# Two-layer decoder trunk on one core: heads and rests of the tokens in one 512-column product

## The chip, the cores and the metric

The kernel runs on one core of one Trainium2 chip. The metric is the device time of one execution in microseconds; the kernel before takes 1001.32 us, the median of three runs (1001.05 to 1001.64).

TensorE (PE in the profile) multiplies: a weight load (PEld) puts a 128x128 stationary operand in place, and a matmul then streams the columns of a moving operand past it into a bank of PSUM. VectorE (DVE), ScalarE (ACT) and GpSimd (POOL) work on tiles; SyncE (SP) and GpSimd issue the transfers from HBM.

## The reference

A trunk of two layers over 512 tokens of 1024 features, all float32. Layer 0 mixes tokens by causal pooling, layer 1 by dilated windowed attention; each is followed by a SwiGLU block, and the end is one more norm.

```python
for i in range(DEPTH):                    # 2
    h = rmsnorm(x, norm_mix[i])
    x = x + (pool_mixer(h, ...) if i % 2 == 0 else attn_mixer(h, ...))
    h = rmsnorm(x, norm_ffn[i])
    x = x + swiglu(h, ffn_w_gate[i], ffn_w_up[i], ffn_w_down[i])
return rmsnorm(x, norm_final)

def swiglu(h, w_gate, w_up, w_down):      # 1024 -> 2816 -> 1024
    g = jnp.einsum('bsd,df->bsf', h, w_gate)
    u = jnp.einsum('bsd,df->bsf', h, w_up)
    return jnp.einsum('bsf,fd->bsd', jax.nn.silu(g) * u, w_down)
```

The change lies in `swiglu`, in both layers.

## The kernel before, in words

**Heads and rests.** A float32 operand is kept as two parts that TensorE takes: the head `hi`, the value rounded, and the rest `lo`, what is left. A product of two operands is three matmuls: head by head, head of the weights by rest of the tokens, rest of the weights by head of the tokens. The weights are split on the chip: `weights` (L120) loads a tile of 128x1024 into `wraw` or `vraw` (L105; L107 adds a second piece in the transfer), casts it on ScalarE (L139) into `whi` and subtracts on VectorE (L143) into `wlo`. Split tiles live in a ring of five (`wspl`), and `weights` keeps about four products ahead. L145 adds raw tiles to each other.

**Seven products instead of eight.** The block of gate and up (1024 features, 512 tokens) is cut in two by two: features in two halves, tokens in two halves of 256. Instead of eight half-size products there are seven, over sums and differences of the quarters of the weights and of the tokens (a scheme like Strassen's, in Winograd's form); `RIGHT[i]` is the tokens' operand of product i. The seven results are combined in three sums: `p` collects products 0, 2, 4 and 6, `r` 1 and 5, `q` 3. `Group` is 256 of the 2816 inner features, gate and up together; there are eleven groups a layer. `Group.product` (L614) runs for g in gate, up and four chunks c of the features the three matmuls of L625, each with 256 columns, one PSUM bank holding gate in one half and up in the other: 24 matmuls. `done` (L632) takes the result out: product 0 to `keep`, 1 and 2 to tile `ct` (ScalarE, L636 to L640), 3, 4, 5 added or subtracted (VectorE, L642 to L646), then SiLU and the multiplication (L647 to L650; L653 and L658 for product 6). `first_half` and `second_half` make from `ct` the seven sums `u` that the down product wants and split them (L320, L321).

**Down.** `down(b)` (L696) takes a block of three groups (`BLOCKS`) through the same seven products, of tokens' halves by halves of the output columns: for two blocks t of 128 tokens each, nine matmuls of 512 columns (L712), 18 a product. After each product VectorE adds the accumulators to the residual stream `x` or subtracts them (L719, L721). The last block of two groups (9, 10) is multiplied plainly (L766).

**The order.** TensorE's order is the order in which the code is written (`manual_schedule`). `FFN_ORDER` gives it: groups 0 and 1 interleaved (`TWO`), groups 2 and 3, down 0, groups 4 to 6, down 1, groups 7 to 9, down 2, group 10, the last block. `enqueue_ffn` puts the weights in a queue in the same order, and loads go out on SP in that order. The other engines' instructions are ordered when the program is built, by priority: what takes results out of PSUM stands ahead (`URGENT`), products 5 and 6 less so (100).

**PSUM.** Four banks rotate under the name `mm`; two each are `p` and `r`, so the next group's `p` and `r` are others than this group's.

Of the kernel before, what the change touches and what calls it, by code (L numbers as in the profile page):

```python
# [10 lines left out]
F32 = mybir.dt.float32  # L11
# [35 lines left out]
FFN_ORDER = (  # L47
    [("two", 0)] + [("quad", n) for n in (2, 3)] + [("down", 0)]
    + [("quad", n) for n in (4, 5, 6)] + [("down", 1)] + [("quad", n) for n in (7, 8, 9)] + [("down", 2)]
    + [("quad", 10)] + [("last", 3)]  # L50
)

TWO = [(g, i) for g in (0, 1) for i in (0, 3)] + [(g, i) for i in (1, 2, 4, 5, 6) for g in (0, 1)]
# [5 lines left out]
def trunk_kernel(ctx: ExitStack, tc: tile.TileContext, x_in, xT, gam, gains, consts, ident_d, w0, wT, w1, wv, w_down, out):  # L59
# [15 lines left out]
    mm = ctx.enter_context(tc.tile_pool(name="mm", bufs=4, space=bass.MemoryType.PSUM))  # L75
# [92 lines left out]
    def enqueue_ffn(layer):  # L168
# [27 lines left out]
        def down(b):  # L196
            pairs = BLOCKS[b]
            at = layer * (NF // 2) + pairs[0]
            dn[b] = [{}, {}]
            for i in range(7):  # L200
                for js, a, n in zip(dn[b], (at, at + 2), (2, len(pairs) - 2)):
                    operand(js, i, lambda m, k: tiles[k, :, a : a + n, COLS[m]], (n, S), 10)

        for step, n in FFN_ORDER:
            if step == "two":
                for g, i in TWO:
                    quad(n + g, i, 5)
            elif step == "quad":
                for i in range(7):
                    quad(n, i)  # L210
            elif step == "down":
                down(n)
            else:
                dn[n] = [rows_of(w_down)(layer * NF + 2 * pair, half) for pair in BLOCKS[n] for half in range(2)]
# [27 lines left out]
    h_both = [stat.tile([P, NC * S + 2 * SHIFT], F32R, name=f"h_{part}") for part in ("hi", "lo")]  # L242

    def tokens_at(shift):
        return [h[:, shift : shift + NC * S].rearrange("p (c s) -> p c s", c=NC) for h in h_both]
# [105 lines left out]
    def out_projection(js, where, hi, lo, norm, shift, four, tps, hook=None):  # L351
# [22 lines left out]
        ws = [weights(js[4 + i], split_ahead=4 + i, load_ahead=6 + i) for i in range(4)]  # L374
        for b in range(4):
# [20 lines left out]
    with ExitStack() as pctx:  # L396
# [137 lines left out]

        third = out_projection(j_out, BY_GROUP, z_hi, z_lo, norm, SHIFT, [mm.tile([P, S], F32, name="mm") for _ in range(4)], turned_banks, lambda: group_products(1, early))

    def ffn(layer, norm, third, nxt):
# [8 lines left out]
        with ExitStack() as fctx:  # L546
# [5 lines left out]
            fps = open_pool("ffps", 2, space=bass.MemoryType.PSUM)  # L552
            early_u = open_pool("ffa", 2)
            third_chain = norm.chain.ins
            h_hi, h_lo = tokens_at(SHIFT)
            block = lambda t, k, n: t[:, 4 * k : 4 * k + 4, HALVES[n]]

# [3 lines left out]
            t2, t3, t4 = ([fp.tile([P, 4, 256], F32R, name=f"t_{part}{i}") for part in ("hi", "lo")] for i in (2, 3, 4))  # L561
            fp.tile([P, SHIFT], F32, name="gap3")
            T_hi, T_lo = ([block(h, 0, 1), t2[i], t3[i], t4[i]] for i, h in enumerate((h_hi, h_lo)))
            RIGHT = (
                [(block(h_hi, 0, 0), block(h_lo, 0, 0))] + [(T_hi[i], T_lo[i]) for i in (0, 1)]
                + [(block(h_hi, 1, 0), block(h_lo, 1, 0)), (T_hi[2], T_lo[2])]
                + [(block(h_hi, 1, 1), block(h_lo, 1, 1)), (T_hi[3], T_lo[3])]
            )
# [12 lines left out]
            class Group:  # L581


                def __init__(self, n, ct):
                    self.n, self.ct, self.sums = n, ct, {}
                    self.lst = ct.rearrange("p m n g c -> p (m n g) c")
                    pool = early_u if n % 4 < 2 else late_u[0]
                    self.u = u_of[n] = [pool.tile([P, 7, 256], F32R, name=t) for t in ("u_hi", "u_lo")]

                def first_half(self):  # L590

                    (hi, lo), lst = self.u, self.lst
# [21 lines left out]
                def product(self, i):  # L614
                    if i == 3:
                        self.sums["q"] = mm.tile([P, S], F32, name="mm").rearrange("p (g c) -> p g c", g=2)
                    elif i < 2:
                        self.sums["pr"[i]] = fps.tile([P, 2, 256], F32, name="pr"[i])
                    ps = self.sums["prpqprp"[i]]
                    whi, wlo = weights(gu[self.n][i])  # L620
                    hi, lo = RIGHT[i]
                    for g in range(2):
                        for c in range(4):
                            for k, (w, xx) in enumerate(((whi, hi), (whi, lo), (wlo, hi))):
                                nc.tensor.matmul(  # L625
                                    ps[:, g, :], lhsT=w[:, g, c, :], rhs=xx[:, c, :],
                                    start=i in (0, 1, 3) and g + c + k == 0, stop=c == 3 and k == 2, skip_group_check=True,
                                )
                    with tc.high_priority(URGENT if i < 5 else 100):
                        self.done(i)  # L630

                def done(self, i):  # L632
# [12 lines left out]
                    elif i == 5:  # L645
                        nc.vector.tensor_add(ct[:, 0, 1], r, ct[:, 0, 1])  # L646
                        nc.scalar.activation(ct[:, 0, :, 0, :], ct[:, 0, :, 0, :], AF.Silu)  # L647
                        nc.vector.tensor_mul(ct[:, 0, :, 0, :], ct[:, 0, :, 0, :], ct[:, 0, :, 1, :])
                        nc.scalar.activation(ct[:, 1, 1, 0, :], ct[:, 1, 1, 0, :], AF.Silu)
                        nc.vector.tensor_mul(ct[:, 1, 1, 0, :], ct[:, 1, 1, 0, :], ct[:, 1, 1, 1, :])  # L650
                        self.first_half()
# [42 lines left out]
            r_tile = lambda: by_four(fps.tile([P, 2, 256], F32, name="r").rearrange("p g c -> p (g c)"))  # L694

            def down(b):  # L696

                pairs = BLOCKS[b]

                p, r = ([fps.tile([P, 2, 256], F32, name=t).rearrange("p g c -> p (g c)") for _ in range(2)] for t in "rp")  # L700
                q = [mm.tile([P, S], F32, name="mm") for _ in range(2)]
                where = (0, 1, 2, 3, 6, 5, 4)
                target = ((0, 0, 1), (1, 1, -1), (0, 1, 1), (0, 0, 1), (1, 1, -1), (0, 1, 1), (1, 0, -1))
                for i, acc in enumerate((p, r, p, q, p, r, p)):
                    ws = [weights(js[i], held=z) for z, js in enumerate(dn[b])]
                    half, n, sign = target[i]
                    for t in range(2):
                        for c, pair in enumerate(pairs):
                            whi, wlo = (w[:, c % 2, :] for w in ws[c // 2])
                            hi, lo = (u[:, where[i], t * P : (t + 1) * P] for u in u_of[pair])  # L710
                            for k, (u, w) in enumerate(((hi, whi), (hi, wlo), (lo, whi))):
                                nc.tensor.matmul(  # L712
                                    acc[t], lhsT=u, rhs=w, start=i in (0, 1, 3) and c + k == 0,
# [3 lines left out]
                        with tc.high_priority(URGENT):  # L717
                            if sign > 0:
                                nc.vector.tensor_add(to, acc[t], to)  # L719
                            else:  # L720
                                nc.vector.tensor_sub(to, to, acc[t])  # L721

            for kind, n in FFN_ORDER[:-1]:
                if kind == "two":
                    groups = [Group(n, ct_common), Group(n + 1, ct_tile(hn, "ct_second"))]
                    with tc.issue_after(third_chain):
                        first_tokens(0, t1r)
                        first_tokens(1, b21r)
                    for at, (g, i) in enumerate(TWO):
                        if at in (0, 2):  # L730
                            b = 2 + at // 2
                            if b == 2:
                                late_banks[b] = third
                                norm.prepare(3, COLS)
                            else:
                                late_banks[b] = [r_tile(), by_four(mm.tile([P, S], F32, name="mm"))]
                                for half in range(2):
                                    norm.turn(b, half, late_banks[b][half])
                            late(b, 1)
                        if at in (4, 6, 8):  # L740
                            for b in (2, 3):
                                late(b, at // 2)
                        groups[g].product(i)
                    held.close()
                    late_u.append(open_pool("ffb", 2))
                elif kind == "quad":
                    group = Group(n, ct_common)
                    for i in range(7):
                        group.product(i)
                else:  # L750
                    down(n)
# [18 lines left out]
            junk = fps.tile([P, 2, 256], F32, name="p").rearrange("p g c -> p (g c)")  # L770
# [476 lines left out]
```

## Time and profile before

| what | value |
|---|---|
| median of three runs | 1001.32 us |
| the profiled execution | 1000.84 us |
| its span, first to last instruction | 999.0 us |
| TensorE matmuls, weight loads | 6575, 6575 |
| TensorE busy | 990.7 us, 99% |
| VectorE busy | 784.6 us, 79% |
| ScalarE busy | 529.5 us, 53% |
| granted TensorE clock | 0.999 |
| feed-forward of layer 0, of layer 1 | about 115 to 450 us, 663 to 999 us |
| gate and up (L625), matmuls in the two layers | 3696, of 256 columns |
| down by blocks (L712), matmuls in the two layers | 756, of 512 columns |

Busy times of matmuls overlap, since matmuls are pipelined: the time that one costs in a row of many is the distance of the starts, not its own length. The chain that ended last gives these distances: a piece such as "x24" is 24 matmuls of one product one behind the other, with its length.

### The profile page before, as it was taken

The numbers are of one execution on the slowest core, as the hardware profiler recorded it, in microseconds if no ns is written. First come the engines' busy times: TensorE is split into PE (matmuls) and PEld (weight loads), VectorE is DVE, ScalarE is ACT, GpSimd is POOL, SyncE is SP. The second block draws the span as 40 slices with busy tenths as digits, with TensorE's granted clock in tenths as the row PEclk, the third lists the DMA queues.
The fourth block names the chain that finished last, engine by engine and source line by source line (L and its number), as shares of the span: only waits on it lengthen the run. The fifth ranks groups of instructions, "written<-read, shape, count | busy, mean of one in ns | idle before, by whom it ended". The sixth has DMA issues, their size and how long they took to land.

```text
span 999.0 us, 16591 instructions
## 1 busy us (share of the span) xinstructions
PE 990.7 (99%) x6575; PEld 908.5 (91%) x6575; DVE 784.6 (79%) x1116; ACT 529.5 (53%) x838; POOL 113.1 (11%) x114
## 2 busy tenths in 40 slices
PE   9999999999999999999999999999999999999997
PEld 8888999989989998989888899899998998999896
DVE  6475799898888888777887557479989889788875
ACT  5573666545644554573543544356654554455354
POOL 0002010110011100002112024101011100111000
PEclk9999999999999999999999999999999999999999
DMA  9457277668559755524211249427666855975522
GB/s 334 177 168 190 60 197 177 151 187 233 149 126 292 182 137 148 183 76 135 83 58 53 62 153 284 92 64 196 174 158 200 234 148 123 289 179 138 155 67 84
DMA packets 76461, 157.29 MB, mean 157 GB/s; under 512 B 5904, under 2 KB 6288, under 8 KB 76384
## 3 DMA queue, kind: packets, MB, share of 16 engines
q1 hardware_dynamic: 58000, 121.00, 36.2%
q0 software_dynamic: 18096, 34.98, 20.3%
q8 instruction: 51, 0.84, 0.3%
q10 hardware_dynamic: 288, 0.27, 0.1%
q14 instruction: 26, 0.21, 0.1%
HBM read 154.08 MB, written 2.13 MB: 156 GB/s over the span
## 4 chain that ended last, share of the span: by engine, by line
PE 97%; ACT 1%; DMA 1%; DVE 1%; POOL 0%; issue 0%; DVEq 0%; ACTq 0%
PE p L625 25%; PE r L625 13%; PE r L712 10%; PE mm L625 6%; PE p L712 5%; PE mm L766 4%; PE mm L227 4%; PE mm L229 4%; PE mm L228 4%; PE mm L712 2%; PE early L443 2%; PE mm L363 2%; PE mm L361 2%; PE mm L362 2%; PE early L490 1%; PE tp L955 1%
## 5 line engine op out<-in xcount | busy, mean ns | idle before, releaser
L139 ACT CAST whi<-wraw 128x1024 fp32r<-128x1024 f32 (+2 forms) x189 | 184.9, 981 | 186.7 <-issue 45.8
L143 DVE TENSOR_TENSOR wlo<-wraw,whi 128x1024 fp32r<-128x1024 f32 (+2 forms) x190 | 221.1, 1165 | 76.2 <-ACT whi L139 75.7
L139 ACT CAST whi<-vraw 128x1024 fp32r<-128x1024 f32 (+1 forms) x102 | 99.6, 977 | 144.8 <-DVE vraw L145 53.7
L625 PE MATMUL p<-t_hi,wlo 128*128 128x256 f32 x528 | 149.8, 284 | 0.0
L625 PE MATMUL p<-t_lo,whi 128*128 128x256 f32 x528 | 149.4, 283 | 0.0
L625 PE MATMUL p<-t_hi,whi 128*128 128x256 f32 x528 | 148.4, 281 | 0.0
L143 DVE TENSOR_TENSOR wlo<-vraw,whi 128x1024 fp32r<-128x1024 f32 (+1 forms) x102 | 114.9, 1127 | 14.0 <-ACT whi L139 13.7
L625 PEld LDWEIGHTS p<-t_hi,whi 128*128 128x128 f32 x528 | 100.0, 189 | 0.0
L625 PE MATMUL r<-h_hi,wlo 128*128 128x256 f32 x352 | 99.9, 284 | 0.0
L625 PEld LDWEIGHTS p<-t_hi,wlo 128*128 128x128 f32 x528 | 99.6, 189 | 0.0
L625 PE MATMUL r<-h_lo,whi 128*128 128x256 f32 x352 | 99.6, 283 | 0.0
L625 PEld LDWEIGHTS p<-t_lo,whi 128*128 128x128 f32 x528 | 99.3, 188 | 0.0
L625 PE MATMUL r<-h_hi,whi 128*128 128x256 f32 x352 | 99.0, 281 | 0.0
L145 DVE TENSOR_TENSOR vraw<-vraw,wraw 128x1024 f32<-128x1024 f32 x68 | 76.6, 1127 | 0.8
L107 POOL DMA_DIRECT2D wraw<-w x22 | 26.7, 1211 | 435.6 <-DVE wlo L143 125.5
L625 PEld LDWEIGHTS r<-h_hi,whi 128*128 128x128 f32 x352 | 66.7, 189 | 0.0
L625 PEld LDWEIGHTS r<-h_hi,wlo 128*128 128x128 f32 x352 | 66.4, 189 | 0.0
L625 PEld LDWEIGHTS r<-h_lo,whi 128*128 128x128 f32 x352 | 66.2, 188 | 0.0
L227 PE MATMUL mm<-h_hi,whi 128*128 128x512 f32 (+1 forms) x176 | 64.8, 368 | 0.0
L229 PE MATMUL mm<-h_hi,wlo 128*128 128x512 f32 (+1 forms) x176 | 63.6, 361 | 0.0
L228 PE MATMUL mm<-h_lo,whi 128*128 128x512 f32 (+1 forms) x176 | 63.5, 361 | 0.0
L712 PE MATMUL r<-whi,u_lo 128*128 128x512 f32 x144 | 56.1, 390 | 0.0
(329 smaller groups left out, 2493.8 us busy)
## 6 DMA issues: line engine op xcount, KB each, us to landing
wraw<-w SPq DMA_DIRECT2D x116, 512.0 KB, 4.7
wraw<-w_down SPq DMA_DIRECT2D x32, 512.0 KB, 3.6
vraw<-w SPq DMA_DIRECT2D x22, 512.0 KB, 5.2
wraw<-w POOLq DMA_DIRECT2D x22, 512.0 KB, 7.6
vraw<-w POOLq DMA_DIRECT2D x22, 512.0 KB, 8.6
wraw<-wT SPq DMA_DIRECT2D x16, 512.0 KB, 4.4
wraw<-w_down SPq DMA_DIRECT2D x24, 256.0 KB, 2.7
vraw<-w_down SPq DMA_DIRECT2D x6, 512.0 KB, 5.5
```

The lines of the kernel that those rows point to most:

```text
L107: nc.gpsimd.dma_start(dst, more, accum_op=ALU.add)
L139: nc.scalar.copy(hi[:, :n], raw[:, :n])
L143: nc.vector.tensor_sub(lo[:, :n], raw[:, :n], hi[:, :n].bitcast(F32))
L145: nc.vector.tensor_add(raws[into][:, :n], raws[into][:, :n], raws[more][:, :n])
L227: nc.tensor.matmul(ps, lhsT=whi, rhs=xhi, start=first, stop=False, **kw)
L228: nc.tensor.matmul(ps, lhsT=whi, rhs=xlo, start=False, stop=False, **kw)
L229: nc.tensor.matmul(ps, lhsT=wlo, rhs=xhi, start=False, stop=last, **kw)
L361: nc.tensor.matmul(ps, lhsT=xhi, rhs=w[0][:, k, :], start=first, stop=False)
L362: nc.tensor.matmul(ps, lhsT=xhi, rhs=w[1][:, k, :], start=False, stop=False)
L625: nc.tensor.matmul(ps[:, g, :], lhsT=w[:, g, c, :], rhs=xx[:, c, :], start=i in (0, 1, 3) and g + c + k == 0, stop=c == 3 and k == 2, skip ...
L712: nc.tensor.matmul(acc[t], lhsT=u, rhs=w, start=i in (0, 1, 3) and c + k == 0, stop=c == len(pairs) - 1 and k == 2, skip_group_check=True,)
L766: nc.tensor.matmul(ps, lhsT=u, rhs=w[:, m, :], start=z + m + k == 0, stop=z == 1 and m == 1 and k == 2,)
```

## The change: what it does

- Heads and rests of the tokens lie in one tile each (`h_both`, `t_both`), so that `right[:, :, k, :]` is 256 columns of heads and 256 of rests.
- In the "paired" groups 2 to 9, products 0, 2, 3, 5 and 6 issue for each g and k one matmul of 512 columns (head of the weights by both), which fills a whole bank, and one of 256 (rest of the weights by the heads) into the bank's first half. Products 1 and 4 still issue three of 256 columns; 1 accumulates into the second half of its banks, 4 into the first. The sum of two halves is the result.
- An accumulator is therefore a pair of banks, gate and up. A group uses three pairs: `a` (M1 and F0 in turn), `q` (M0) and `c` (F1). Product 0 goes to `a` and is copied to `q`; product 2 is added to `a`, which is copied to `c`; product 3 is added in `q`, 1 and 5 in `c`, 4 and 6 in `a`.
- `paired_done` takes the results out: of products 3, 5 and 6 the second half is copied by ScalarE to `ct` and the first is added or subtracted by VectorE; of 1 ScalarE copies the second half; of 4 VectorE subtracts the first half. SiLU of product 6 now follows its combination.
- `Down` uses a pair for `p` (the one of M1 and F0 that is free), F1 for `r` and M0 for `q`. The first product is copied from `p` to `q` by ScalarE and not added to `x`; the fourth accumulates on the copy, and is added to `x` with it.
- `PLAN` replaces `FFN_ORDER`, product by product: in a paired group 0, then 5 and 6 of the group before, then 2, 3, 1, 4; down 0 to 2 come one product ahead of the third, sixth and ninth group's end (before 5 and 6), and the next group's 0 stands before down's last product. The weights are queued in the order of `PLAN`, but 1, 2, 3, 4 of a group in this order.
- Groups 0, 1 and 10 keep the products of before. The rotation of `mm` banks is written out (`Ring`), with the starting bank set in places.

```diff
+BODY, USED = (1, 2, 3, 4), (2, 3, 1, 4)
+PAIRED = range(2, 10)
+def _plan():
+    first = lambda n: [("quad", n, 0)] if n in PAIRED else []
+    steps = TWO[:-1] + first(2) + TWO[-1:]
+    for n in PAIRED:
+        steps += [("quad", n, i) for i in USED]
+        ends = [("quad", n, 5), ("quad", n, 6)]
+        if n % 3 == 0:
+            b = n // 3 - 1
+            steps += [("down", b, 0)] + ends + [("down", b, i) for i in range(1, 6)] + first(n + 1) + [("down", b, 6)]
+        else:
+            steps += first(n + 1) + ends
+    return steps + [("one", 10, i) for i in range(7)] + [("last", 3, 0)]
...
+                    if self.pairs:
+                        a, q, c = self.pairs
+                        to = (a, c, a, q, a, c, a)[i]
+                        for g in range(2):
+                            for k in range(4):
+                                w, rest, more = whi[:, g, k, :], wlo[:, g, k, :], dict(skip_group_check=True)
+                                if i in (1, 4):
+                                    at = to[:, g, HALVES[i == 1]]
+                                    nc.tensor.matmul(at, lhsT=w, rhs=right[:, 0, k, :], start=False, stop=False, **more)
+                                    nc.tensor.matmul(at, lhsT=w, rhs=right[:, 1, k, :], start=False, stop=False, **more)
+                                else:
+                                    at = to[:, g, HALVES[0]]
+                                    both = to[:, g, :].rearrange("p (z c) -> p z c", z=2)
+                                    nc.tensor.matmul(both, lhsT=w, rhs=right[:, :, k, :], start=i == 0 and k == 0, stop=False, **more)
+                                nc.tensor.matmul(at, lhsT=rest, rhs=right[:, 0, k, :], start=False, stop=k == 3, **more)
...
+                def paired_done(self, i):
+                    ct = self.ct
+                    a, q, c = self.pairs
+                    own, more = HALVES
+                    if i == 0:
+                        nc.scalar.copy(q, a)
+                    elif i == 2:
+                        nc.scalar.copy(c, a)
+                    elif i == 3:
+                        nc.scalar.copy(ct[:, 0, 0], q[:, :, more])
+                        nc.vector.tensor_add(ct[:, 0, 0], q[:, :, own], ct[:, 0, 0])
+                    elif i == 1:
+                        nc.scalar.copy(ct[:, 1, 1], c[:, :, more])
+                    elif i == 4:
+                        nc.vector.scalar_tensor_tensor(
+                            ct[:, 1, 1], a[:, :, own], -1.0, ct[:, 1, 1], op0=ALU.mult, op1=ALU.subtract
+                        )
+                    elif i == 5:
+                        nc.scalar.copy(ct[:, 0, 1], c[:, :, more])
+                        nc.vector.tensor_add(ct[:, 0, 1], c[:, :, own], ct[:, 0, 1])
+                        self.gate_first()
+                    elif i == 6:
+                        nc.scalar.copy(ct[:, 1, 0], a[:, :, more])
+                        nc.vector.scalar_tensor_tensor(
+                            ct[:, 1, 0], a[:, :, own], -1.0, ct[:, 1, 0], op0=ALU.mult, op1=ALU.subtract
+                        )
+                        nc.scalar.activation(ct[:, 1, 0, 0, :], ct[:, 1, 0, 0, :], AF.Silu)
+                        nc.vector.tensor_mul(ct[:, 1, 0, 0, :], ct[:, 1, 0, 0, :], ct[:, 1, 0, 1, :])
+                        self.second_half()
...
+                                nc.tensor.matmul(
+                                    acc, lhsT=u, rhs=w, start=i in (0, 1) and c + k == 0,
...
+                            if i == 0:
+                                nc.scalar.copy(self.q[:, t, :], acc)
+                            elif sign > 0:
+                                nc.vector.tensor_add(to, acc, to)
...
+                    if i == 0:
+                        downs[n] = Down(n, spare_pairs[0], F1, M0)
+                        spare_pairs.reverse()
...
+                if i == 0 and kind == "quad":
+                    groups[n] = Group(n, ct_common, (spare_pairs[0], M0, F1))
+                    spare_pairs.reverse()
...
+                groups[n].product(i, held={1: -2, 2: 1, 3: 1}.get(i, 0) if kind == "quad" else 0)
```

More of the change, by code (lines that the diff above doesn't have):

```diff
@@ L46 @@
 BLOCKS = ((0, 1, 2), (3, 4, 5), (6, 7, 8), (9, 10))
[L47 to L53, printed above, removed]
+TWO = [("one", g, i) for g in (0, 1) for i in (0, 3)] + [("one", g, i) for i in (1, 2, 4, 5, 6) for g in (0, 1)]
+BODY, USED = (1, 2, 3, 4), (2, 3, 1, 4)
[12 more added lines that the diff above has]
+    return steps + [("one", 10, i) for i in range(7)] + [("last", 3, 0)]
+PLAN = _plan()
 TOKENS = np.arange(S).reshape(J, R).T.reshape(-1)
@@ L74, in trunk_kernel, with __init__, tile @@
     tmp = ctx.enter_context(tc.tile_pool(name="tmp", bufs=1))
-    mm = ctx.enter_context(tc.tile_pool(name="mm", bufs=4, space=bass.MemoryType.PSUM))
+    mm_banks = ctx.enter_context(tc.tile_pool(name="mm", bufs=1, space=bass.MemoryType.PSUM)).tile([P, 4, S], F32, name="mm")
+    class Ring:
+        def __init__(self, *banks):
+            self.banks, self.at = banks, 0
+        def tile(self, *_, **__):
+            self.at += 1
+            return self.banks[(self.at - 1) % len(self.banks)]
+    mm = Ring(*(mm_banks[:, i, :] for i in range(4)))
     ctx.enter_context(tc.manual_schedule(engines={PE}))
@@ L194, in enqueue_ffn, with down @@
         tiles = w_down.rearrange("(n k p) c -> k p n c", k=2, p=P)
-        def down(b):
+        def down(b, i):
             pairs = BLOCKS[b]
             at = layer * (NF // 2) + pairs[0]
[L199 to L209, printed above, removed]
+            for js, a, n in zip(dn.setdefault(b, [{}, {}]), (at, at + 2), (2, len(pairs) - 2)):
+                operand(js, i, lambda m, k: tiles[k, :, a : a + n, COLS[m]], (n, S), 10)
+        for kind, n, i in PLAN:
+            if kind == "one":
+                quad(n, i, 5 if n < 2 else 10)
+            elif kind == "quad":
+                if i == USED[0]:
+                    for each in BODY:
+                        quad(n, each)
+                elif i not in BODY:
                     quad(n, i)
-            elif step == "down":
-                down(n)
+            elif kind == "down":
+                down(n, i)
             else:
@@ L241, in trunk_kernel, with tokens_both @@
     stat.tile([P, 32], F32, name="gap0")
-    h_both = [stat.tile([P, NC * S + 2 * SHIFT], F32R, name=f"h_{part}") for part in ("hi", "lo")]
+    h_both = stat.tile([P, 2, NC * S + 2 * SHIFT], F32R, name="h")
+    def tokens_both(shift):
+        return h_both[:, :, shift : shift + NC * S].rearrange("p z (c s) -> p z c s", c=NC)
     def tokens_at(shift):
-        return [h[:, shift : shift + NC * S].rearrange("p (c s) -> p c s", c=NC) for h in h_both]
+        both = tokens_both(shift)
+        return [both[:, z] for z in range(2)]
     stat.tile([P, 40], F32, name="gap1")
@@ L551, in ffn @@
             fp = open_pool("ffn", 1)
-            fps = open_pool("ffps", 2, space=bass.MemoryType.PSUM)
+            fps = open_pool("ffps", 1, space=bass.MemoryType.PSUM)
+            F0, F1 = (fps.tile([P, 2, S], F32, name=f"f{i}") for i in range(2))
+            M0, M1 = mm_banks[:, 0:2, :], mm_banks[:, 2:4, :]
+            by_g = lambda t: t.rearrange("p (g c) -> p g c", g=2)
+            fp_ring, fr_ring = (Ring(t[:, 0, :], t[:, 1, :]) for t in (F0, F1))
             early_u = open_pool("ffa", 2)
@@ L612, in second_half, with product @@
                     split(hi[:, 2:7, :], lo[:, 2:7, :], lst[:, 3:8, :])
-                def product(self, i):
+                def product(self, i, held=0):
+                    whi, wlo = weights(gu[self.n][i], held=held)
+                    right = RIGHT[i]
+                    if self.pairs:
[13 more added lines that the diff above has]
+                                nc.tensor.matmul(at, lhsT=rest, rhs=right[:, 0, k, :], start=False, stop=k == 3, **more)
+                        with tc.high_priority(URGENT if i < 5 else 100):
+                            self.paired_done(i)
+                        return
@@ L615, in product @@
                     if i == 3:
[L616 removed]
+                        self.sums["q"] = by_g(mm.tile())
                     elif i < 2:
[L618 removed]
+                        self.sums["pr"[i]] = by_g((fp_ring, fr_ring)[i].tile())
                     ps = self.sums["prpqprp"[i]]
[L620 removed]
@@ L693, in ffn, with __init__, product @@
             by_four = lambda t: t.rearrange("p (j t) -> p j t", j=4)
[L694 to L705, printed above, removed]
+            r_tile = lambda: by_four(fr_ring.tile())
+            class Down:
+                def __init__(self, b, p, r, q):
+                    self.b, self.accs, self.p, self.q = b, (p, r, p, q, p, r, p), p, q
+                def product(self, i):
+                    pairs, js = BLOCKS[self.b], dn[self.b]
+                    where = (0, 1, 2, 3, 6, 5, 4)
+                    target = ((0, 0, 1), (1, 1, -1), (0, 1, 1), (0, 0, 1), (1, 1, -1), (0, 1, 1), (1, 0, -1))
+                    ws = [weights(j[i], held=z) for z, j in enumerate(js)]
                     half, n, sign = target[i]
                     for t in range(2):
+                        acc = self.accs[i][:, t, :]
                         for c, pair in enumerate(pairs):
@@ L717, in down @@
                         with tc.high_priority(URGENT):
-                            if sign > 0:
-                                nc.vector.tensor_add(to, acc[t], to)
-                            else:
[L721 to L743, printed above, removed]
@@ new lines, in ffn @@
+            for at, (kind, n, i) in enumerate(PLAN[:-1]):
+                if at in (0, 2):
+                    b = 2 + at // 2
+                    if b == 2:
+                        late_banks[b] = third
+                        norm.prepare(3, COLS)
+                    else:
+                        late_banks[b] = [r_tile(), by_four(mm_banks[:, 3, :])]
+                        for half in range(2):
+                            norm.turn(b, half, late_banks[b][half])
+                    late(b, 1)
+                if at in (4, 6, 8):
+                    for b in (2, 3):
+                        late(b, at // 2)
+                if kind == "down":
+                    if i == 0:
+                        downs[n] = Down(n, spare_pairs[0], F1, M0)
+                        spare_pairs.reverse()
+                    downs[n].product(i)
+                    continue
+                if i == 0 and kind == "quad":
+                    groups[n] = Group(n, ct_common, (spare_pairs[0], M0, F1))
+                    spare_pairs.reverse()
+                elif n == 10 and i == 0:
+                    groups[n] = Group(n, ct_common)
+                groups[n].product(i, held={1: -2, 2: 1, 3: 1}.get(i, 0) if kind == "quad" else 0)
+                if (n, i) == (1, 6):
@@ L768, in products @@
                         )
[L770 removed]
+            junk = fp_ring.tile()
             def close(b, half, ps, quarter=None):
```

56 lines of the change are left out of this document (30 added, 26 removed).

## The prediction

> **What bounds the kernel now.** I read the profile's page first (engine shares, the 40 slices, the chain that ended last), then the chain piece by piece through the two feed-forward stages, then the engines' busy time by stage.
>
> ```profile
> span 999.0 us, 16591 instructions
> PE 990.7 (99%) x6575; PEld 908.5 (91%) x6575; DVE 784.6 (79%) x1116; ACT 529.5 (53%) x838; POOL 113.1 (11%) x114
> PEclk9999999999999999999999999999999999999999
> PE 97%; ACT 1%; DMA 1%; DVE 1%; POOL 0%; issue 0%; DVEq 0%; ACTq 0%
> ```
>
> TensorE carries 97% of the chain at full granted clock, and there is one weight load for each matmul (6575 of each). In the feed-forward stages the chain is nothing but products, one behind the other, without a hole:
>
> ```profile
> 193.10 2.85 PE p L625 x24
> 195.95 4.11 PE r L712 x18
> 200.06 4.08 PE p L712 x18
> ...
> 224.54 2.88 PE p L625 x24
> 227.42 2.88 PE r L625 x24
> 230.30 2.88 PE p L625 x24
> 233.18 2.88 PE mm L625 x24
> ...
> 241.82 5.76 PE p L625 x48
> ```
>
> A gate-and-up product is 24 matmuls of 256 columns in 2.88 us, so 120.0 ns from start to start (118.8 ns in groups 0 to 3: 2.85 us). A down product is 18 matmuls of 512 columns in 4.08 us, 226.7 ns each. Twice 120.0 is 240.0: two matmuls of 256 columns take 13.3 ns more than one of 512. By these two rows a column costs (226.7 - 120.0)/256 = 0.417 ns, and each matmul pays 13.3 ns beside its columns. A third size, 320 columns (the attention's values), fits: from the first to the last row below 14 rounds of three matmuls take 6.16 us, 146.7 ns each, against 320 x 0.417 + 13.3 = 146.7.
>
> ```profile
> 594.96 0.15 PE mm L1129
> ...
> 601.12 0.15 PE mm L1129
> ```
>
> So only work taken from TensorE moves the end here, and a wait put in front of it costs its full length.
>
> **The change, part by part.**
>
> (a) *Fewer matmuls.* In the 16 paired groups (2 to 9, two layers) products 0, 2, 3, 5 and 6 take 16 matmuls instead of 24: eight pairs of 256 + 256 become eight of 512, the eight with the weights' rests stay at 256. Products 1 and 4 keep 24 of 256. That is 40 matmuls and 40 weight loads less a group, 640 in all. A group from 4 on: before 168 x 120.0 = 20.16 us; after 40 x (226.7 + 120.0) + 48 x 120.0 = 19.63 us; -0.53 us, and 12 of them -6.4 us. Groups 2 and 3 run today at 118.8, 19.95 us; that pace is seen only ahead of the first 512-column product, so I give them 19.63 after too: -0.32 us, 4 of them -1.3 us. Sum -7.7 us.
>
> The mixed stream (512, 256, 512, ...) is not in the trace. The nearest rows are the switches between the two sizes:
>
> ```profile
> 224.38 0.28 PE L625 MATMUL p<-h_hi,whi 128*128 128x256 f32 x1
> 224.50 0.28 PE L625 MATMUL p<-h_lo,whi 128*128 128x256 f32 x1
> 224.62 0.28 PE L625 MATMUL p<-h_hi,wlo 128*128 128x256 f32 x1
> ...
> 284.85 0.39 PE L712 MATMUL r<-whi,u_hi 128*128 128x512 f32 x1
> 285.09 0.40 PE L712 MATMUL r<-wlo,u_hi 128*128 128x512 f32 x1
> 285.32 0.40 PE L712 MATMUL r<-whi,u_lo 128*128 128x512 f32 x1
> ...
> 286.94 0.39 PE L712 MATMUL r<-whi,u_hi 128*128 128x512 f32 x1
> ```
>
> After a run of 256 columns the first nine of 512 take 2.09 us (284.85 to 286.94) instead of 9 x 0.2267 = 2.04: a spell of 0.05 us, after which the pace is 226.7. The other way there is no loss (0.12 us at once). One end: the spell comes once for each run of 256 columns, that is once a group behind products 1 and 4, 16 x 0.05 = 0.8 us. Other end: it never ends, and every 512 takes the 0.235 us of the first two rows: 640 x 8.3 ns = 5.3 us. I take the first, because the spell ends in 2 us in the row and a mixed stretch lasts five products. A gain here, a 256 behind a 512 at 116.5 ns as in some of these starts, would be 640 x 3.5 ns = 2.2 us; kept as the far end. (a) is worth -6.9 us, between -2.4 and -9.9.
>
> The page "TensorE: Matmul & The Clock Gate" of the Trainium skill ("Wait — 56ns, not 53.3ns?") speaks against this: it gives warm start-to-start as N / 2.4 GHz plus about 2.5 ns, 215.7 ns for 512 columns. By it 640 matmuls less would be worth 640 x 2.5 = 1.6 us, an estimate from that page. The trace disagrees at all three sizes (226.7 ns at 512, 13.3 over the columns), and I go by the trace.
>
> (b) *More ScalarE work a group, some more on VectorE.* Products 0 and 2 now copy two banks (1024 columns) instead of one; products 3, 5 and 6 each get a copy of the rests' half; product 6's subtraction and SiLU now go over both gate and up, with a multiply from SBUF.
>
> ```profile
> L139 ACT CAST whi<-wraw 128x1024 fp32r<-128x1024 f32 x12 | 12.6, 1050 | 7.1 <-PE p L625 3.4 <-issue 1.3 <-PE r L625 1.2
> L636 ACT COPY keep<-p 128x512 f32<-128x512 f32 x3 | 1.7, 583 | 0.2 <-PE p L625 0.2
> L139 ACT CAST whi<-wraw 128x512 fp32r<-128x512 f32 x1 | 0.6, 622 | 1.3 <-PE mm L625 1.3
> L644 DVE SCALAR_TENSOR_TENSOR ct<-p,ct 128x512 f32<-128x512 f32 x3 | 2.1, 686 | 1.6 <-PE p L625 1.6
> L650 DVE TENSOR_TENSOR ct<-ct 128x256 f32<-128x256 f32 x3 | 1.3, 419 | 0.0
> L658 DVE SCALAR_TENSOR_TENSOR ct<-p,ct 128x256 f32<-128x256 f32 x2 | 0.8, 420 | 0.0
> ```
>
> A 1024-column copy from PSUM to PSUM is not in the trace; 583 + (1050 - 622) = 1011 ns is my estimate from these rows (two copies of 583 would be 1166). ScalarE: 2 x 428 + 3 x 583 = 2.6 us a group more. VectorE: 686 + 419 - 420 = 0.69 us more.
>
> ```profile
> 196.00:224.50 28.50, 28.50 (x128) 23.58 (x127) 26.15 (x35) 13.37 (x16) 4.49 (x4) 1.00 0.64 185
> 224.50:285.00 60.50, 60.50 (x506) 60.50 (x505) 49.83 (x58) 34.22 (x45) 6.91 (x6) 1.00 0.75 188
> 663.00:703.50 40.50, 40.50 (x345) 40.50 (x344) 39.85 (x56) 28.36 (x43) 3.62 (x3) 1.00 0.62 176
> ```
>
> (Columns: stage, length, busy PE, weight load, VectorE, ScalarE, GpSimd, clock, DMA share, GB/s.) Three groups occupy VectorE for 49.8 of 60.5 us; after, 51.9 of 58.9, 88%. ScalarE goes from 34.2 to 42.0, 71%. The third row, groups 0 and 1, runs with VectorE at 98% and TensorE without a hole, so 88% by itself stops nothing. I cost (b) at nothing, covered by TensorE's 19.6 us a group.
>
> (c) *Down's fourth product on a copy of the first.* Two VectorE adds of 0.69 us are replaced by two ScalarE copies of 583 ns a block; in the down stage VectorE falls from 26.2 to about 24.8 us. Off the path: 0.
>
> (d) *PSUM handed on more tightly.* Pair F1 is now c for every group, and the accumulator of down's products 1 and 5. Two waits are new. First: product 2 ends, ScalarE copies a to c, and product 1 accumulates on c; only product 3 lies between, 8 x (226.7 + 120.0) = 2.77 us. What delays such copies today:
>
> ```profile
> 227.45 0.59 ACT L636 COPY keep<-p 128x512 f32<-128x512 f32 x1 [0.24 <-PE p L625]
> 231.22 0.57 ACT L638 COPY ct<-r 128x512 f32<-128x512 f32 x1
> 249.19 1.27 ACT L320 CAST u_hi<-ct 128x1280 fp32r<-128x1280 f32 x1
> 250.42 1.05 ACT L139 CAST whi<-wraw 128x1024 fp32r<-128x1024 f32 x1
> 252.08 0.59 ACT L638 COPY ct<-r 128x512 f32<-128x512 f32 x1 [0.61 <-DVE u_lo L321]
> ```
>
> They start 0.03 us (227.42) to 0.92 us (230.30) after the next product, behind one weight cast; so the copy ends 1.0 to 1.9 us after product 2, before 2.77. Cost 0; without that cover, what exceeds 2.77. Second: down's product 1 starts on F1 one product (2.77 us) after the group's product 5, whose ScalarE copy (0.03 to 0.92 late, 0.58) and then VectorE add (0.69, behind up to one 1.22 us subtraction) must be over: 1.3 to 3.4 us, so 0 to 0.6 us, six times: 0 to 3.8. I take 0, its middle (2.35) being inside.
>
> (e) *The order of the products* (0, then the previous group's 5 and 6, then 2, 3, 1, 4). Weights are still queued 1, 2, 3, 4, so product 1's buffer is freed late, and the fifth tile behind it, product 5's, has two products (2.88 + 2.77 = 5.65 us) for its cast (1.05) and subtraction (1.22) where others have four; down's products, with two tiles of the five each, live on a comparable margin today. Loads leave SP in the new order with the same ten items ahead. Cost 0; stalls here belong to the slower rival's kind.
>
> Sum: -6.9 us. The profiled execution took 1000.84 us (span 999.0), so 993.9 for such a one; on the median of 1001.32, **994.4 us**.
>
> **The rivals.**
>
> *1. Some hand-overs bite* (d at its far end, 3.8 us): -3.1 us, 998.2. For it: the reach to 3.4 us above; against: it needs all delays together.
>
> *2. The mixed stream stays in the spell*, or the fixed cost is not saved whole: 235 + 120 a pair saves 5 ns in 480 pairs, 2.4 us, and about 0.2 in the other 160: 998.7. For it: every second matmul is a switch. Against: the spell ends while 512s are fed. The 2.5 ns of the Trainium skill's page named above would give 999.7, in the same place.
>
> *3. It does not do what it says:* the 512 columns are read in two runs of 256, heads and rests lying apart, and every 512-column matmul in the trace reads one run. Were a run paid like a matmul, nothing is saved: 1001.3. Against it speaks only that no row shows a price for a run.
>
> *4. Slower: the copy to c comes late in each group.* ScalarE takes its instructions in order. The copy at 252.08 above waits for the split of the previous group's u, 1.6 us behind the end of its product (247.58 + 2.88 = 250.46). If the copy to c is queued behind such a waiting instruction and a cast, it ends at 1.6 + 1.05 + 1.01 + 0.2 for the product's drain = 3.9 us, 1.1 us over 2.77; 16 groups: 17.6 us, 1012. It outweighs the gain from 6.9/16 = 0.43 us a group. For it: ScalarE at 71%, product 6's longer chain ahead of the split. Against: the copies of products 0 and 2 do not write what the split reads, and none comes later than 0.93 us today.
>
> **How the numbers follow.** Forecast 0.70 (its own range 992.0 to 996.5), rival 1 0.09, rival 2 0.06, rival 3 0.04, rival 4 0.11. About 0.2% (2.0 us) is what a measurement tells from no change: faster is below 999.3, slower above 1003.3. Faster: 0.70 + 0.09 + 0.04 of rival 2 = 0.83. Same: 0.02 + 0.04 + 0.02 of a mild rival 4 = 0.08. Slower 0.09. The range runs from 991.5 ((a) at its far end) to 999.5 and leaves out rivals 3 and 4 with a little of the rest, under 0.2.
>
> **What would show it.** TensorE 5935 matmuls; in the chain, mixed products of 16 in 2.77 us and none above 2.85; products 1 and 4 at 2.88. Starts of 512s inside a mixed product at 227, not 235. Copies to c ended before product 1 starts. VectorE about 52 us in three groups. I am wrong if holes stand in front of product 1, of down's product 1 or of product 5, or if a mixed product takes over 2.85 us.

## The result

The changed kernel takes 1246.89 us (median of four runs, 1244.78 to 1247.65), the kernel before 1001.18 in the same runs: a ratio of 1.2452 with a 95% interval of 1.243 to 1.2473. 994.4 had been predicted. The change makes the kernel a quarter slower.

The page of the changed kernel, the lines that answer to those shown of before:

```profile
span 1244.8 us, 15419 instructions
PE 1051.3 (84%) x5935; PEld 890.5 (72%) x5935; DVE 798.6 (64%) x1120; ACT 572.2 (46%) x898; POOL 113.8 (9%) x114
PEclk9899999999999999997988998999999999999999
PE 9%; DVE 2%; issue 1%; ACT 1%; ACTq 0%
```

TensorE has its 640 matmuls less (5935) and is now busy 84% of the span instead of 99%. No other engine has taken the lead: VectorE is at 64%. The chain of releasers, which went through TensorE for 97% of the span before, can be followed for some 13% only. The list of TensorE's waits tells why (who waits, for whom, total us, times, longest): 150 waits of 186.9 us in all after, 3 of 1.9 us before. Before, over the whole kernel:

```profile
PE mm L261 <- DVE odd_rows L255: 1.1, 1, 1.1
PE mm L1129 <- DVE v L1135: 0.5, 1, 0.5
PE mm L1129 <- ACT ropea L1115: 0.3, 1, 0.3
```

and after, the longest of 37 lines:

```profile
PE mm L800 <- DVE x L809: 31.6, 24, 1.7
PE mm L800 <- DVE x L811: 14.6, 12, 1.7
PE mm L250 <- DVE ropea L956: 13.0, 9, 5.6
PE mm L250 <- DVE e L1001: 12.6, 3, 4.6
PE mm L664 <- ACT f L691: 12.2, 6, 2.3
PE mm L862 <- DVE x L376: 9.9, 13, 0.8
PE mm L250 <- DVE u_lo L499: 8.4, 2, 6.7
PE mm L250 <- DVE e L1031: 8.1, 2, 5.1
```

Every waiting matmul in these lines writes `mm`, and the third, fourth, seventh and eighth lie in the attention and in the pooling mixer, where the change has no new order and no merged product. What they wait for is an instruction that reads an `mm` bank. In detail, one hole between two down products (L800; starts, durations, idle before):

```profile
250.07 0.40 PE L800 MATMUL mm<-whi,u_lo 128*128 128x512 f32 x1
251.95 0.47 PE L800 MATMUL mm<-whi,u_hi 128*128 128x512 f32 x1 [1.48 <-DVE x L809]
```

```profile
250.51 0.69 DVE L166 TENSOR_TENSOR wlo<-wraw,whi 128x512 fp32r<-128x512 f32 x1 [1.04 <-ACT whi L162]
251.11 0.69 DVE L809 TENSOR_TENSOR x<-mm,x 128x512 f32<-128x512 f32 x1
```

The matmul at 251.95 opens down's fourth product, which accumulates in the pair M0. It waits until VectorE has added the last bank of the third product, a bank of the pair M1, to `x` (251.11 + 0.69 = 251.80). Start to start that is 1.88 us where 0.23 is the pace. The sum it waits for and the sum it begins have no bank in common.

### The profile page after: what moved, and what is told of

Same layout as the page of the kernel before. It is cut to its first block, busy times and chain, and to the rows that moved or that the text cites. A ratio compares the mean times of both kernels' runs of the same rounds, so it can differ in the third digit from the quotient of the medians.

```text
span 1244.8 us, 15419 instructions
## 1 busy us (share of the span) xinstructions
PE 1051.3 (84%) x5935; PEld 890.5 (72%) x5935; DVE 798.6 (64%) x1120; ACT 572.2 (46%) x898; POOL 113.8 (9%) x114
## 5 line engine op out<-in xcount | busy, mean ns | idle before, releaser
L162 ACT CAST whi<-wraw 128x1024 fp32r<-128x1024 f32 (+2 forms) x189 | 184.0, 979 | 295.6 <-issue 75.6
L166 DVE TENSOR_TENSOR wlo<-vraw,whi 128x1024 fp32r<-128x1024 f32 (+1 forms) x102 | 115.2, 1129 | 66.3 <-ACT whi L162 66.2
L800 PE MATMUL mm<-whi,u_hi 128*128 128x512 f32 x180 | 75.2, 418 | 54.5 <-DVE x L809 31.6
L250 PE MATMUL mm<-h,whi 128*128 128x512 f32 (+1 forms) x176 | 71.7, 408 | 33.9 <-DVE ropea L956 13.0
L665 PE MATMUL f<-h,wlo 128*128 128x256 f32 x336 | 95.0, 283 | 0.0
L800 PEld LDWEIGHTS mm<-whi,u_hi 128*128 128x128 f32 x180 | 33.7, 187 | 78.8 <-ACT whi L162 22.6
L664 PE MATMUL mm<-h,whi 128*128 128x512 f32 x176 | 66.8, 415 | 16.4 <-ACT f L691 12.2
L664 PE MATMUL f<-h,whi 128*128 128x512 f32 x208 | 73.8, 394 | 0.0
L800 PE MATMUL mm<-whi,u_lo 128*128 128x512 f32 x180 | 70.6, 392 | 0.0
L800 PE MATMUL mm<-wlo,u_hi 128*128 128x512 f32 x180 | 70.6, 392 | 0.0
L251 PE MATMUL mm<-h,whi 128*128 128x512 f32 (+1 forms) x176 | 69.1, 393 | 0.0
L252 PE MATMUL mm<-h,wlo 128*128 128x512 f32 (+1 forms) x176 | 68.7, 391 | 0.0
L665 PE MATMUL f<-t,wlo 128*128 128x256 f32 x240 | 67.9, 283 | 0.0
L665 PEld LDWEIGHTS f<-h,wlo 128*128 128x128 f32 x336 | 63.3, 188 | 0.4
L664 PE MATMUL f<-t,whi 128*128 128x512 f32 x160 | 57.0, 394 | 0.0
```

Of the source, the lines that this page charges most:

```text
L162: nc.scalar.copy(hi[:, :n], raw[:, :n])
L166: nc.vector.tensor_sub(lo[:, :n], raw[:, :n], hi[:, :n].bitcast(F32))
L250: nc.tensor.matmul(ps, lhsT=whi, rhs=xhi, start=first, stop=False, **kw)
L251: nc.tensor.matmul(ps, lhsT=whi, rhs=xlo, start=False, stop=False, **kw)
L252: nc.tensor.matmul(ps, lhsT=wlo, rhs=xhi, start=False, stop=last, **kw)
L664: nc.tensor.matmul(both, lhsT=w, rhs=right[:, :, k, :], start=i == 0 and k == 0, stop=False, **more)
```

## The experiments

What I held after this: the four rotating banks had become slices of one tile, and the waits that are set when the program is built go by the tile, not by the bank; so a matmul into one bank waits for the readers of the others (false waits). The rivals: the new order of the products, the tighter hand-over of F1, and the instructions that read two banks at once.

**The one tile alone, on the kernel before.**

```diff
-    mm = ctx.enter_context(tc.tile_pool(name="mm", bufs=4, space=bass.MemoryType.PSUM))
+    mm_banks = ctx.enter_context(tc.tile_pool(name="mm", bufs=1, space=bass.MemoryType.PSUM)).tile([P, 4, S], F32, name="mm")
+    mm = Ring(*(mm_banks[:, i, :] for i in range(4)))
```

> The kernel before, with nothing changed but that its four rotating banks are one tile of four banks. False waits: the stages outside the feed-forward get what they got in the changed kernel (25 us ahead of the first feed-forward, 83 us in the attention), and the feed-forward, where product 3, down's fourth product and the last block use these banks, some 20 us: 1110 to 1140 us. Rival (the time comes from the new order and hand-overs): 1001 us.

1133.22 us, ratio 1.132 (1.1304 to 1.1335). Not one matmul differs from before, and 132 us are added. Its three longest waits in the attention are those of the changed kernel, to a tenth:

```profile
PE mm L237 <- DVE ropea L870: 13.0, 9, 5.6
PE mm L237 <- DVE e L915: 12.6, 3, 4.6
PE mm L237 <- DVE e L945: 8.1, 2, 5.1
```

**A tile for each bank, on the changed kernel.** Everything else stays: the merged products, the order, the copies, one tile for heads and rests. What was one instruction over a pair becomes one for each bank (shortened, "..." stands for what is left out, here and below).

```diff
-    mm_banks = ... .tile([P, 4, S], F32, name="mm")
+    mm_banks = [mm_pool.tile([P, S], F32, name=f"mm{i}") for i in range(4)]
...
-    mm = Ring(*(mm_banks[:, i, :] for i in range(4)))
+    mm = Ring(*mm_banks)
...
-            F0, F1 = (fps.tile([P, 2, S], F32, name=f"f{i}") for i in range(2))
-            M0, M1 = mm_banks[:, 0:2, :], mm_banks[:, 2:4, :]
+            F0, F1 = ([fps.tile([P, S], F32, name=f"f{i}{g}") for g in range(2)] for i in range(2))
+            M0, M1 = mm_banks[0:2], mm_banks[2:4]
...
-                        nc.scalar.copy(c, a)
+                            nc.scalar.copy(c[g], a[g])        # for g in range(2), and so for each instruction
```

> The changed kernel with each PSUM bank a tile of its own: a pair is a list of two banks, and what one ScalarE or VectorE instruction took out of a pair is two instructions, one a bank. Theory (false waits: a matmul waits for the readers of another bank because the banks are one tile): the 245 us go, and the time is that of the prediction's sum, 993 to 999 us. Rival (the waits are real: the new order, the tighter hand-over of F1, the order of ScalarE's queue): the feed-forward stages keep most of their excess of about 140 us, 1120 us or more.

996.58 us, ratio 0.9959 (0.9946 to 0.9971): 250 us less than the changed kernel and 0.4% faster than before. TensorE waits as little as before. The lines of its page and its whole list of waits:

```profile
span 994.9 us, 15598 instructions
PE 986.7 (99%) x5935; PEld 876.3 (88%) x5935; DVE 794.0 (80%) x1184; ACT 578.4 (58%) x994; POOL 113.1 (11%) x114
PE 97%; ACT 1%; DMA 1%; DVE 1%; POOL 0%; issue 0%; DVEq 0%; ACTq 0%
```

```profile
PE mm L289 <- DVE odd_rows L283: 1.1, 1, 1.1
PE mm L1230 <- DVE v L1236: 0.3, 1, 0.3
PE mm L1230 <- ACT ropea L1216: 0.3, 1, 0.3
```

There is no wait left in the feed-forward. So the hand-over of F1, the copies to c and q and the new order hold TensorE up nowhere once the false waits are gone.

**The tile or the instructions over two banks?** The last kernel had lost both. Here its split instructions stay, and the banks are slices of large tiles again.

```diff
-    mm_banks = [mm_pool.tile([P, S], F32, name=f"mm{i}") for i in range(4)]
+    mm_all = ... .tile([P, 4, S], F32, name="mm")
+    mm_banks = [mm_all[:, i, :] for i in range(4)]
...
-            F0, F1 = ([fps.tile([P, S], F32, name=f"f{i}{g}") for g in range(2)] for i in range(2))
+            F0, F1 = ([t[:, g, :] for g in range(2)] for t in [fps.tile([P, 2, S], F32, name=f"f{i}") for i in range(2)])
```

> The kernel with a tile per bank, with every instruction as it is there (one for each bank), but the banks again slices of one tile of four and two tiles of two. It tells the tile from the instruction that reads two banks at once, which also went. If the tile makes the waits: as the changed kernel, 1230 to 1260 us. If the pair-wide instructions made them: 997 us.

1260.53 us in one run. The same instructions on the same banks take 997 or 1261 us, by what is declared a tile. This kernel is 14 us slower than the changed one, which has one instruction where this one has two. About half of that stands in the lists of waits: those for the copies from a to c and from a to q are 23.5 us here and 16.5 there.

**Two tiles of two banks.**

```diff
+    mm_pairs = [mm_pool.tile([P, 2, S], F32, name=f"mm{i}") for i in range(2)]
...
-    mm = Ring(*(mm_banks[:, i, :] for i in range(4)))
+    mm = Ring(*(mm_pairs[i // 2][:, i % 2, :] for i in range(4)))
...
-            M0, M1 = mm_banks[:, 0:2, :], mm_banks[:, 2:4, :]
+            M0, M1 = mm_pairs
```

> The changed kernel with the four banks as two tiles of two banks instead of one of four. False waits: those between the two pairs go, those inside a pair stay. Down's two token blocks share a pair (about 13 us a block of groups, 76 us in all stay), the paired groups' own 4 to 5 us a stage go, and outside the feed-forward, where the banks rotate, every second false wait stays (about 54 of 108 us): near 1120 us. Real waits: no change, 1247 us.

1146.72 us in one run: 100 us go, 150 over the tile per bank stay. The direction is as expected, the size 27 us off. By the stages below, 57 us stay outside the feed-forward, near the 54 expected, but 93.5 in it and not 76: I had left out the unpaired groups 0, 1 and 10, whose `p` and `r` rotate through the halves of F0 and F1 and wait on each other inside the pair. Their lines (`PE f L678`) add up to 13.4 us in the list, so they explain most of those 17.5; two of them, beside down's (L801):

```profile
PE mm L801 <- DVE x L812: 17.5, 12, 1.9
PE mm L801 <- DVE x L810: 15.5, 12, 1.7
...
PE f L678 <- ACT ct L731: 3.1, 2, 1.6
PE f L678 <- ACT ct_second L731: 3.1, 2, 1.5
```

The line of the paired products that waited 12.2 us (`PE mm L664 <- ACT f L691`, the copy from a to c) has no counterpart among this kernel's waits. In the changed kernel one such place reads:

```profile
198.00 1.01 ACT L691 COPY f<-mm 128x1024 f32<-128x1024 f32 x1
...
199.06 0.50 PE L664 MATMUL mm<-h,whi 128*128 128x512 f32 x1 [2.25 <-ACT f L691]
```

a is M1 there, and the matmul opens product 3 in M0: with the two pairs in one tile it waited for a copy out of the other pair. Of the 16 copies from a to c in the changed kernel, 6 read M1 and 10 read F0, and product 3 waited for just the 6.

**F0 and F1 a tile per bank, `mm` still one tile.**

```diff
-            F0, F1 = (fps.tile([P, 2, S], F32, name=f"f{i}") for i in range(2))
-            M0, M1 = mm_banks[:, 0:2, :], mm_banks[:, 2:4, :]
+            F0, F1 = ([fps.tile([P, S], F32, name=f"f{i}{g}") for g in range(2)] for i in range(2))
+            M0, M1 = ([mm_banks[:, z + g, :] for g in range(2)] for z in (0, 2))
...
```

The instructions are again one for each bank.

> The changed kernel with the four banks of the feed-forward's own two pairs as tiles of their own, and the four rotating banks still one tile. False waits: the stages outside the feed-forward stay as in the changed kernel (140 us ahead of it, 296 us attention); in the feed-forward the waits on F0 and F1 go (about 14 us in down, 13 us in the products), 1215 to 1225 us. If these waits were real hand-overs of F1, no change: 1247 us.

1228.68 us in one run, 18 us less than the changed kernel, somewhat short of the 22 to 32 expected. The nearer comparison is the kernel of 1260.53 us, which has the same split instructions on large tiles: against it, tiles of their own for F0 and F1 save 32 us (one run of each). Outside the feed-forward little changes (140.4 us ahead of it, 292.5 in the attention).

Where the time lies, by stage (lengths in us, from the profiled executions):

| kernel | ahead of the first feed-forward | first feed-forward | attention | second feed-forward to the end | span |
|---|---|---|---|---|---|
| before | 115.1 | 331.0 | 216.7 | 336.2 | 999.0 |
| changed | 140.4 | 399.0 | 295.6 | 409.8 | 1244.8 |
| before, one tile | 140.7 | 343.7 | 290.2 | 354.4 | 1129.0 |
| changed, split instructions, large tiles | 141.0 | 407.1 | 295.2 | 415.4 | 1258.7 |
| changed, F0 and F1 per bank | 140.4 | 391.4 | 292.5 | 402.6 | 1226.9 |
| changed, two tiles of two | 123.4 | 373.6 | 265.6 | 382.4 | 1145.0 |
| changed, a tile per bank | 115.2 | 328.6 | 217.2 | 333.9 | 994.9 |

104 of the 246 us lie in the stages that the change doesn't speak of (25.3 and 78.9), and the one tile alone gives almost all of these. The feed-forward's other 142 come from false waits of both kinds, across the pairs and inside one. Some of it is the clock; the attention's row of before and of after, whose third column from the end is the granted clock:

```profile
446.10:662.80 216.70, 215.98 (x1342) 188.39 (x1340) 149.43 (x271) 95.43 (x234) 40.59 (x47) 1.00 0.40 112
```

```profile
539.40:835.00 295.60, 243.17 (x1342) 203.76 (x1340) 150.00 (x268) 95.58 (x235) 41.56 (x47) 0.92 0.28 81
```

With holes of up to 5.6 us in this stage it is 0.92 instead of 1.00, for the same 1342 matmuls; 0.08 of 295.6 us, 24 us, is my estimate of the most that this can explain of the stage's 78.9. The Trainium skill's page "TensorE: Matmul & The Clock Gate" ("Why this matters for your kernels") warns that the clock drops to half where TensorE idles for more than about 3 us. This trace agrees in the drop to half: the clock is 0.50 from 566.7 to 573.5 us, where a hole of 5.6 us ends at 568.01. It does not agree in the 3 us as a bound. In the second feed-forward, behind a hole of 1.97 us, the clock is 0.50 for 3.4 us:

```profile
897.07 0.50 PE L664 MATMUL mm<-h,whi 128*128 128x512 f32 x1 [1.97 <-ACT f L691]
```

```profile
897.80:901.20 3.40, 3.40 (x13) 2.92 (x12) 1.49 (x1) 0.41 (x1) 0.00 (x0) 0.50 0.94 208
```

Not every such hole does it: from 146 to 530 us, with holes of up to 2.3 us, the clock stays at 1.00.

**What the merging is worth.** The kernel with a tile per bank, and the 512 columns issued as two matmuls of 256:

```diff
-    nc.tensor.matmul(both, lhsT=w, rhs=right[:, :, k, :], start=i == 0 and k == 0, stop=False, **more)
+    nc.tensor.matmul(both[:, 0, :], lhsT=w, rhs=right[:, 0, k, :], start=i == 0 and k == 0, stop=False, **more)
+    nc.tensor.matmul(both[:, 1, :], lhsT=w, rhs=right[:, 1, k, :], start=False, stop=False, **more)
```

> As the kernel with a tile per bank, but each matmul of 512 columns issued as two of 256 into the bank's halves: 640 matmuls more. By the prediction's step (a), 6.9 us (2.4 to 9.9) more than that kernel; if merging saves nothing, the same time.

1001.36 us, ratio 1.0006 (0.9997 to 1.0015), so 4.8 us more than with 512 columns. In the trace the two feed-forwards up to their last matmul differ by 5.3 us: first this kernel, then the one with 512 columns.

```profile
115.10:446.30 331.20, 331.20 (x2347) 312.27 (x2346) 286.99 (x401) 211.66 (x330) 32.94 (x29) 1.00 0.64 169
663.10:992.90 329.80, 329.80 (x2345) 311.40 (x2343) 286.01 (x401) 207.54 (x326) 33.26 (x29) 1.00 0.61 164
```

```profile
115.20:443.80 328.60, 328.60 (x2028) 296.00 (x2026) 287.35 (x401) 211.90 (x330) 32.95 (x29) 1.00 0.64 170
661.00:988.10 327.10, 327.10 (x2025) 295.09 (x2022) 286.20 (x401) 208.08 (x326) 33.24 (x29) 1.00 0.61 165
```

That is 8.3 ns for each of the 640 matmuls saved (5.3/640), not 13.3. The rest of the change (new order, copies, one down add less) can't be told from nothing, taken together: this kernel against before is 1.0006 with 1 inside the interval. The mixed stream in the kernel with 512 columns:

```profile
229.87 0.39 PE L665 MATMUL mm<-h,whi 128*128 128x512 f32 x1
230.09 0.28 PE L666 MATMUL mm<-h,wlo 128*128 128x256 f32 x1
230.22 0.40 PE L665 MATMUL mm<-h,whi 128*128 128x512 f32 x1
230.45 0.28 PE L666 MATMUL mm<-h,wlo 128*128 128x256 f32 x1
...
232.32 0.40 PE L665 MATMUL mm<-h,whi 128*128 128x512 f32 x1
...
232.68 0.28 PE L660 MATMUL f<-h,whi 128*128 128x256 f32 x1
```

Seven pairs take 2.45 us (229.87 to 232.32), 350.0 ns each, where 226.7 + 120.0 = 346.7, and the product of eight pairs takes 2.81 (to 232.68). The 512s take between 0.22 and 0.24; over all 640 of them in the trace the mean is 230.6 ns.

**What makes a 512 slower there?** Two experiments on the kernel with a tile per bank. First the eight 512s of a product ahead of its eight 256s:

```diff
+    for g in range(2):
+        for k in range(4):
+            nc.tensor.matmul(both, lhsT=whi[:, g, k, :], rhs=right[:, :, k, :], start=i == 0 and k == 0, ...)
+    for g in range(2):
+        for k in range(4):
+            nc.tensor.matmul(to[g][:, HALVES[0]], lhsT=wlo[:, g, k, :], rhs=right[:, 0, k, :], start=False, ...)
```

> The kernel with a tile per bank, but in a mixed product the eight matmuls of 512 columns stand first and the eight of 256 behind them, instead of one and one in turn. With a tile per bank the 512s took 230.5 ns in the mean in turn with 256s, not 226.7. If every 512 that follows a 256 pays the 3.8 ns (cost of a switch), only one in eight still pays: 560 x 3.8 ns = 2.1 us less, 994.5 us. If a spell runs over the first nine 512s behind any run of 256s, nothing is gained: 996.6 us.

995.83 us, ratio 0.9952 (0.994 to 0.9965); the interval overlaps that of the kernel in turn, and the feed-forwards are 0.8 us shorter in the trace (328.2 and 326.7). Two products, the first right behind a down product (L814):

```profile
226.53 0.39 PE L814 MATMUL mm<-wlo,u_hi 128*128 128x512 f32 x1
226.76 0.39 PE L814 MATMUL mm<-whi,u_lo 128*128 128x512 f32 x1
226.98 2.02 PE L660 MATMUL f<-t,whi 128*128 128x512 f32 x8
228.84 1.12 PE L663 MATMUL f<-t,wlo 128*128 128x256 f32 x8
229.79 2.02 PE L660 MATMUL mm<-h,whi 128*128 128x512 f32 x8
231.65 1.10 PE L663 MATMUL mm<-h,wlo 128*128 128x256 f32 x8
```

Eight 512s in a row take 1.86 us, 232.5 ns each, in both products. So it isn't the single 512 behind each switch of size that pays. But a spell behind a run of 256s isn't the whole answer either: the first eight stand right behind 18 matmuls of 512 columns, whose pace is 0.23 up to the last, and are as slow. Of the 80 products, 14 follow a down product like this, and their 512s take 232.3 ns in the mean. The 256s in a row take 0.95 us (228.84 to 229.79), and the product 2.81 (226.98 to 229.79), just as with the sizes in turn. Then the 512 columns are read in one run, from heads alone; this kernel leaves out the tokens' rests and sums in the 512s, so its output is another:

```diff
-    nc.tensor.matmul(both, lhsT=w, rhs=right[:, :, k, :], start=i == 0 and k == 0, stop=False, **more)
+    nc.tensor.matmul(to[g], lhsT=w, rhs=h_z[:, 0, k, :], start=i == 0 and k == 0, stop=False, **more)
```

> The kernel with a tile per bank, but the 512 columns of a mixed product are read in one run, from heads alone, instead of 256 heads and 256 rests that lie apart; so the products of the paired groups are made of other numbers and the output is not the reference's. If the two runs cost the 3.8 ns a matmul, the 512s go to 226.7 ns and the time to 994.1 us. If the switch between the sizes costs it, nothing changes: 996.6 us.

997.34 us (995.21 to 997.72), ratio 0.9958 (0.9944 to 0.9971), and in the trace both feed-forwards to a tenth as long as with two runs:

```profile
115.10:443.70 328.60, 328.60 (x2028) 295.87 (x2027) 287.30 (x401) 212.13 (x330) 32.95 (x29) 1.00 0.64 171
662.00:989.10 327.10, 327.10 (x2025) 294.96 (x2023) 286.19 (x401) 208.16 (x326) 33.25 (x29) 1.00 0.62 165
```

Reading heads and rests from two places costs nothing that these runs show.

## Why the prediction was wrong

**The step that failed** is (d), "PSUM handed on more tightly", with its sentence "Two waits are new". It looked only for matmuls that wait for readers of the same bank, and the whole sum rested on that. The two waits that it named did cost nothing, even in the changed kernel: no product 1 of a paired group is in its list of waits, and the first block of down's product 1 opens without a hole. But the change also made one tile of the four rotating banks, and one of each pair F0 and F1. I had described this myself, as a rotation that "is written out", and gave it no term at all, so no rival covered it either. The runs put in its place: 150 waits of TensorE, 186.9 us in the list, nearly all for readers of another bank of the tile, since 3 waits are left with a tile per bank. They are worth 250 us, the distance between these two kernels, with the slower clock and what else follows a wait; how the other 63 us divide is open. On the kernel before, the one tile alone adds 132 us.

**Rival 4** forecast the right sign by a mechanism that doesn't exist here. The copy to c is late for nobody that needs it: product 1 never waits for it. In the changed kernel that copy does stand in the list of waits, but product 3 waits for it, which goes to another pair.

**(a)** had the right mechanism and the wrong size. 640 matmuls less are worth 4.8 us by the times and 5.3 by the trace, not 6.9; inside the bounds of 2.4 to 9.9. The mis-sized term is the spell of slower 512s: I let it end within a group, at 0.8 us in all, and the 512s stay at 230.6 ns on average through the mixed stretch, 640 x 3.9 ns = 2.5 us. That a run of 256s brings the spell on was my reading of one place, and the products that directly follow 512s are against it. Rival 2 named this (235 ns in every pair) and overstated it. By the 2.5 ns a matmul of the Trainium skill's page the estimate was 1.6 us; the runs are against it, as the trace was.

**(b), (c), (e)** stand: with 256-column matmuls, a tile per bank and all the rest of the change the time is that of before. The copy of 1024 columns from PSUM to PSUM takes 1.01 us as estimated (the row at 198.00 above); ScalarE got its additional work (187.6 to 211.9 us in the first feed-forward) and held nobody up. **Rival 1** is excluded, since no wait on F1 is left with a tile per bank; **rival 3** as well, since one run of columns costs what two do.

Of the signs that I had named, the 5935 matmuls came. Holes came too, but not where I had named them: none in front of a group's products 1 and 5 or of down's product 1, but in front of product 3, and above all between and inside down's products. Without the false waits a mixed product takes 2.81 us, between the 2.77 forecast and the limit of 2.85.

## What to carry to other kernels

When separate buffers become slices of one, look up what the program's waits go by: here by the PSUM tile, so banks that are used in rotation must be tiles of their own, even at the price of one instruction more for each bank. If the list of waits shows an engine waiting in stages that a change did not touch, look for what these stages share with it, a buffer's declaration first. And a saving measured on a uniform stream must be measured again in the mixed stream that the change makes: here 8.3 ns a matmul instead of 13.3.

## What the runs showed of the hardware

Matmuls of 512 columns do not always keep the pace of 226.7 ns that down's products settle at: in the paired products they take 230.6 ns in turn with 256s and 232.5 when eight stand in a row, also right behind a down product. The product takes 2.81 us either way. Why is open: the switch of size and, in turn with 256s, the reading in two runs are excluded; nothing else was tried.

The TensorE clock fell to half behind a hole of 5.6 us, but also behind one of only 1.97 us, while others of up to 2.3 us left it at full.
